# An encoder layer on one core: pair products interleaved, half weight tiles, no full-width GpSimd work, and the switch moved inside attention

## The chip, the cores and the metric

The kernel runs on one core of a Trainium2 chip, in one launch. The metric is the device time in microseconds (us). Five engines take part: PE (TensorE, matrix products into PSUM banks), DVE (VectorE), ACT (ScalarE), POOL (GpSimd) and SP (SyncE, which here only issues transfers). Each works through its own instructions in the order in which the program lists them.

## What is computed

Two sequences of 1024 tokens and 1024 features go through one encoder layer each, in float32. Cut to what matters:

```python
h = rmsnorm(x, norm_g) * (1.0 + scale) + shift          # scale, shift, gate = split(silu(c) @ w_ada + b_ada)
a_b, a_c, a_x, a_z, q, k, v, b_z, lr_f, lr_b, m_a, m_b = split(h @ w_in)
u   = depthwise_conv(a_c * a_x, conv_w, conv_b)
y_a = (a_b * u * silu(a_z)) @ w_a_out
g_f, g_b = log_sigmoid(lr_f @ w_gate_f + b_gate_f) / 16, log_sigmoid(lr_b @ w_gate_b + b_gate_b) / 16
o   = gla(q, k, v, g_f, strict=False) + flip(gla(flip(q), flip(k), flip(v), flip(g_b), strict=True))
y_b = (rmsnorm_per_head(o) * gla_norm_g * silu(b_z)) @ w_b_out
out = rmsnorm(x + gate * ((sigmoid(m_a) * y_a + sigmoid(m_b) * y_b) @ w_out), final_norm_g)
```

## The kernel before, in words

Activations stand transposed: 128 features on the partitions, tokens in the free dimension. A float32 product is made of three: each operand is split into a rounded high part and the rest (`split`, L120: ACT writes the high part, L122, DVE subtracts, L123), and high by high, high by low and low by high are summed in PSUM. One matrix product is then 128x128 weights by 512 tokens.

For each sequence `s` the stages follow each other. `start` (sequence 0 alone) makes the normalised input with the first three projections and ends with `sums` and `sum_parts` of all four activation tiles; `first_conv` finishes their convolution. For sequence 1 `refill` makes the input during the merge before it. `projections` runs **pair jobs**: `fast` (L230) makes two 128-column weight tiles by all tokens with the seven products of the Winograd form of Strassen's scheme, 12 matmuls each. `stationary` (L183) makes the seven stationary operands (six by `split`, the second by L206 to L210) on ACT and DVE, four products ahead (`AHEAD`); in sequence 0 each is also stored to DRAM by SP (L190), and sequence 1 loads it from there (`loaded`, L219). The seven products go to three banks a, b, c in the order a, c, b, a, b, b, c, and five DVE additions (L274, L280, L281, L284, L287) and two ACT copies (L272, L276) read the banks. A raw weight tile of 512 KB takes one of three slots, an operand one of four. Fourteen or sixteen jobs a sequence are convolution channels (`conv_jobs`: C, X, Z, B), where POOL makes the products of `silu` (L637, L649, L673); ten are queries, keys, values and gates, and beside these run `low_ranks` and `decays` (PE, then four ACT functions, each with a table load, L821 to L827) and a third task (`prepare` or `gate_rows`). `small` tiles of 4 KB a partition share seven slots.

`mixers` (L740) runs attention for four heads and fills PE with ordinary products (`halves`): first the 20 of `gates`, spread over three heads; at the start of the fourth `run(dense)` ends them, and `first_out` begins, whose activation `b` `reload` (L1004) brings from DRAM and splits, and spreads its eight products over that head. In attention POOL subtracts the low part of the queries (`Qs`, L919). `merge` multiplies by `w_b_out` (POOL adds at L1024), `final` by `w_out` (POOL subtracts for `mg`). A scheduler sets the order on each engine from the dependences, the slots and the place in the code.

Of the kernel before, what the change touches and what calls it, by code (L numbers as in the profile page):

```python
# [11 lines left out]
F32 = mybir.dt.float32  # L12
# [5 lines left out]
P = 128  # L18
# [17 lines left out]
NBIG, NSMALL, NW, NRAW = 18, 7, 4, 3  # L36
# [21 lines left out]
def encoder_kernel(ctx, tc, x_p, x_s, x_t, weights, w_lr, w_gate, w_out, vectors, b_gate, final_norm_g, masks, y_p, y_s):  # L58
# [52 lines left out]
    r1_d = dram.tile([P, L], F32, name="r1_d")  # L111
    gb_d = dram.tile([2, P, D], F32, name="gb_d")

    def staged(src, shape=(P, L), queue=lambda load: None):

        raw = sb.tile(list(shape), F32, name="raw", tag="raw", bufs=NRAW)
        queue(nc.sync.dma_start(out=raw, in_=src))
        return raw
# [7 lines left out]
    def load_w(i, w=None, **kw):  # L126

        with tc.high_priority(offset=30):
            raw = staged(weights[i].rearrange("p (k c) -> p k c", c=P), (P, KT, P), **kw)
            parts = []  # L130
            for half in range(2):
                t = sb.tile([P, 2, 4, P], F32R, name="w", tag="w", bufs=NW) if w is None else w[:, half]
                split(t[:, 0], t[:, 1], raw[:, 4 * half:4 * half + 4], nc.vector)
                parts.append(t)
        return lambda k: (parts[k // 4][:, 0, k % 4, :], parts[k // 4][:, 1, k % 4, :])
# [47 lines left out]
    def stationary(load, keep=None):  # L183
# [4 lines left out]
        def kept(t, n):  # L188
            if keep is not None:
                nc.sync.dma_start(out=kept_d[keep, n], in_=t.bitcast(F32).rearrange("p a c -> p (a c)"))  # L190
            return t
# [13 lines left out]
        x = sb.tile([P, 4 * P], F32, name="s1", tag="s1", bufs=2)  # L205
# [7 lines left out]
        yield parts(a12, 3)  # L213
        nc.vector.tensor_sub(out=a12, in0=a12, in1=a11)
        yield parts(a21, 4)
# [3 lines left out]
    def loaded(keep):  # L219

        yield None
        for n in range(7):
            if n % 2:
                t = sb.tile([P, 2, 4 * P], F32R, name="wk", tag="raw", bufs=NRAW)
            else:
                t = sb.tile([P, 2, 4 * P], F32R, name="w", tag="w", bufs=NW)
            nc.sync.dma_start(out=t.bitcast(F32).rearrange("p a c -> p (a c)"), in_=kept_d[keep, n])
            yield t

    def fast(jobs, mv):  # L230

        ops = []

        def make():
            later = iter(())
            for n, (load, _, _) in enumerate(jobs):
                gen = later if n else load()
                if not n:  # L240
                    next(gen)
                for i in range(7):
                    if i == 2 and n + 1 < len(jobs):
                        later = jobs[n + 1][0]()
                        next(later)
                    ops.append(next(gen))
                    yield
                next(gen, None)

        maker = make()  # L250
        for load, place, there in jobs:
            banks = {}
            for i, (o, first) in enumerate(((B11, True), (0, True), (1, True), (B21, False), (2, False), (3, False),
                                            (B22, False))):
                while len(ops) < AHEAD[load.ready]:
                    if next(maker, 0) == 0:
                        break
                if first:
                    banks["acb"[i]] = dense_ps()
                a, b, c = (banks.get(n) for n in "abc")  # L260
                ps = banks["acbabbc"[i]]
                w = ops.pop(0)
                for k in range(4):
                    (mhi, mlo), cs = mv.operand(o, k), slice(k * P, (k + 1) * P)

                    nc.tensor.matmul(ps, w[:, 0, cs], mhi, start=(first and k == 0), stop=False, skip_group_check=True)  # L266
                    nc.tensor.matmul(ps, w[:, 0, cs], mlo, start=False, stop=False, skip_group_check=True)  # L267
                    nc.tensor.matmul(ps, w[:, 1, cs], mhi, start=False, stop=(k == 3), skip_group_check=True)  # L268
                if i == 0:
                    keep = small("keep", shape=(P, 2, HALF))  # L270
                    p1, u2 = keep[:, 0, :], keep[:, 1, :]
                    nc.scalar.copy(out=p1, in_=a)  # L272
                elif i == 2:
                    nc.vector.tensor_add(out=u2, in0=b, in1=p1)  # L274
                elif i == 3:
                    nc.scalar.copy(out=place(0, 0), in_=a)  # L276
                    there(0, 0)
                elif i == 4:
                    d = place(1, 1)
                    nc.vector.tensor_add(out=d, in0=b, in1=p1)  # L280
                    nc.vector.tensor_add(out=d, in0=c, in1=d)  # L281
                    there(1, 1)
                elif i == 5:
                    nc.vector.tensor_add(out=place(1, 0), in0=b, in1=p1)  # L284
                    there(1, 0)
                elif i == 6:
                    nc.vector.tensor_add(out=place(0, 1), in0=c, in1=u2)  # L287
                    there(0, 1)
                yield
# [874 lines left out]
```

## Time and profile before

| what | value |
|---|---|
| median of 3 runs | 2523.21 us (2519.05 to 2525.99) |
| the profiled execution's own time | 2527.07 us |
| its span | 2525.3 us |
| PE busy | 2355.0 us (93%), 10993 matmuls |
| DVE, ACT, POOL busy | 1439.7, 999.3, 312.2 us |
| mean granted clock of PE | 0.968 |
| DMA moved | 464.70 MB, mean 184 GB/s |

A matmul of 512 columns shows some 0.4 us, but they are pipelined, so the time from one start to the next is shorter; what PE loses is read from its idle time, the granted clock, and the count of matmuls in a stretch.

### The profile page before, as it was taken

The numbers are of one execution on the slowest core, as the hardware profiler recorded it, in microseconds if no ns is written. First come the engines' busy times: TensorE is split into PE (matmuls) and PEld (weight loads), VectorE is DVE, ScalarE is ACT, GpSimd is POOL, SyncE is SP. The second block draws the span as 40 slices with busy tenths as digits, with TensorE's granted clock in tenths as the row PEclk, the third lists the DMA queues.
The fourth block names the chain that finished last, engine by engine and source line by source line (L and its number), as shares of the span: only waits on it lengthen the run. The fifth ranks groups of instructions, "written<-read, shape, count | busy, mean of one in ns | idle before, by whom it ended". The sixth has DMA issues, their size and how long they took to land.

```text
span 2525.3 us, 28803 instructions
## 1 busy us (share of the span) xinstructions
PE 2355.0 (93%) x10993; PEld 1916.8 (76%) x10993; DVE 1439.7 (57%) x1895; ACT 999.3 (40%) x1579; POOL 312.2 (12%) x187
## 2 busy tenths in 40 slices
PE   7799988989999998999999998998999997999998
PEld 4677766767788876887788886777778886888887
DVE  5866765667766575667732333434857566644333
ACT  6532222786444444343310112772444444332221
POOL 2210110001100100012101110010010000003431
PEclk8899999999999998899999999999999998999999
DMA  6256655768714233437366664777432415358531
GB/s 236 74 218 245 242 208 208 267 253 315 284 64 150 88 122 140 161 134 274 125 199 209 203 209 155 255 252 267 184 115 101 152 67 208 107 202 289 184 127 67
DMA packets 145898, 464.70 MB, mean 184 GB/s; under 512 B 13760, under 2 KB 38944, under 8 KB 142688
## 3 DMA queue, kind: packets, MB, share of 16 engines
q1 hardware_dynamic: 122144, 377.25, 43.3%
q10 hardware_dynamic: 23616, 85.60, 8.6%
q8 instruction: 87, 1.43, 0.2%
q14 instruction: 51, 0.42, 0.1%
HBM read 280.87 MB, written 181.93 MB: 183 GB/s over the span
## 4 chain that ended last, share of the span: by engine, by line
PE 65%; ACT 8%; DVE 8%; DMA 8%; issue 8%; POOL 2%; ACTq 0%; SPq 0%; DVEq 0%; POOLq 0%
PE ps L141 10%; PE ps L143 10%; PE ps L142 10%; PE ps L266 9%; PE ps L268 8%; PE ps L267 8%; DMA raw<-in_weights_dram 4%; PE pl L854 3%; PE pm L141 1%; PE pm L142 1%; PE pm L143 1%; DMA qk<-q_d 1%; DVE w L123 1%; PE ps L788 1%; DMA x<-in_x_t_dram 1%
## 5 line engine op out<-in xcount | busy, mean ns | idle before, releaser
L122 ACT CAST w<-raw 128x512 fp32r<-128x512 f32 x306 | 185.7, 619 | 296.0 <-PE ps L143 108.7
L123 DVE TENSOR_TENSOR w<-raw,w 128x512 fp32r<-128x512 f32 x306 | 231.2, 765 | 119.2 <-ACT w L122 117.3
L141 PE MATMUL ps<-hi,w 128*128 128x512 f32 x688 | 275.4, 402 | 15.0 <-ACT pr L728 9.5
L143 PE MATMUL ps<-hi,w 128*128 128x512 f32 x688 | 274.3, 399 | 0.2 <-DVE w L123 0.2
L142 PE MATMUL ps<-lo,w 128*128 128x512 f32 x688 | 273.3, 397 | 0.0
L266 PE MATMUL ps<-th,w 128*128 128x512 f32 x608 | 247.9, 408 | 25.3 <-DVE single L280 10.9
L268 PE MATMUL ps<-th,w 128*128 128x512 f32 x608 | 243.7, 401 | 12.6 <-DVE w L210 10.9
L267 PE MATMUL ps<-tl,w 128*128 128x512 f32 x608 | 242.9, 399 | 0.0
L141 PE MATMUL ps<-b,w 128*128 128x512 f32 x512 | 204.7, 400 | 12.2 <-ACT w L122 11.4
L266 PE MATMUL ps<-hi,w 128*128 128x512 f32 x504 | 198.2, 393 | 7.9 <-ACT w L122 3.0
L142 PE MATMUL ps<-b,w 128*128 128x512 f32 x512 | 202.9, 396 | 0.0
L143 PE MATMUL ps<-b,w 128*128 128x512 f32 x512 | 200.9, 394 | 0.0
L268 PE MATMUL ps<-hi,w 128*128 128x512 f32 x504 | 196.4, 392 | 1.4 <-DVE w L123 1.4
L267 PE MATMUL ps<-lo,w 128*128 128x512 f32 x504 | 197.6, 392 | 0.1
L266 PEld LDWEIGHTS ps<-th,w 128*128 128x128 f32 x608 | 118.0, 194 | 62.7 <-DVE single L280 15.4
L141 PEld LDWEIGHTS ps<-hi,w 128*128 128x128 f32 x688 | 131.1, 191 | 41.0 <-ACT pr L728 9.9
L143 PEld LDWEIGHTS ps<-hi,w 128*128 128x128 f32 x688 | 131.0, 190 | 26.5 <-DVE w L123 0.6
L142 PEld LDWEIGHTS ps<-lo,w 128*128 128x128 f32 x688 | 131.2, 191 | 24.0
L268 PEld LDWEIGHTS ps<-th,w 128*128 128x128 f32 x608 | 117.4, 193 | 41.8 <-DVE w L210 13.8
L267 PEld LDWEIGHTS ps<-tl,w 128*128 128x128 f32 x608 | 118.2, 194 | 24.0
L141 PEld LDWEIGHTS ps<-b,w 128*128 128x128 f32 x512 | 98.0, 191 | 32.7 <-ACT w L122 12.4
L266 PEld LDWEIGHTS ps<-hi,w 128*128 128x128 f32 x504 | 95.2, 189 | 31.3 <-ACT keep L272 5.0
(271 smaller groups left out, 4687.4 us busy)
## 6 DMA issues: line engine op xcount, KB each, us to landing
kept_d<-w SPq DMA_DIRECT2D x168, 512.0 KB, 3.3
raw<-in_weights_dram SPq DMA_DIRECT2D x128, 512.0 KB, 5.1
w<-kept_d SPq DMA_DIRECT2D x96, 512.0 KB, 4.2
wk<-kept_d SPq DMA_DIRECT2D x72, 512.0 KB, 4.0
g_d<-sg ACTq DMA_DIRECT2D x32, 512.0 KB, 2.7
g<-g_d SPq DMA_DIRECT2D x32, 512.0 KB, 5.4
araw<-in_weights_dram SPq DMA_DIRECT2D x16, 512.0 KB, 4.3
ta_d<-u ACTq DMA_DIRECT2D x16, 512.0 KB, 2.9
```

Source lines behind the costliest of these rows:

```text
L122: high = nc.scalar.copy(out=hi, in_=raw)
L123: engine.tensor_sub(out=lo, in0=raw, in1=hi.bitcast(F32))
L141: nc.tensor.matmul(out, ahi, bhi, start=(first and i == 0), stop=False)
L142: nc.tensor.matmul(out, ahi, blo, start=False, stop=False)
L143: nc.tensor.matmul(out, alo, bhi, start=False, stop=(last and i == n - 1))
L266: nc.tensor.matmul(ps, w[:, 0, cs], mhi, start=(first and k == 0), stop=False, skip_group_check=True)
L267: nc.tensor.matmul(ps, w[:, 0, cs], mlo, start=False, stop=False, skip_group_check=True)
L268: nc.tensor.matmul(ps, w[:, 1, cs], mhi, start=False, stop=(k == 3), skip_group_check=True)
L788: nc.tensor.matmul(ps[:4 * RANK], w[:, k, :], h, start=(k + i == 0), stop=(k * i == KT - 1))
L854: nc.tensor.matmul(pl[:, j * P:(j + 1) * P], km[:, c * P:(c + 1) * P], qm(c), start=True, stop=True)
```

## The change

1. `fast`: the products of neighbouring jobs alternate. In the steady state P1 and P5 of job n are followed by P4 of job n-1, P6 of n, P3 of n-1, P2 and P7 of n. P1, P6, P7 and P4 use one bank, P5 and P3 another, P2 a third; P1 has its bank from `psl`, two banks that attention used alone. Three DVE additions and four ACT copies are left for each job; two 512-wide `keep` tiles stand outside `small`, which has six slots.
2. Raw tiles are half as large (256 KB) in six slots; each half of a weight tile is its own transfer.
3. The products of `silu`, `Ql`, the low part of `mg` and the sum at L1024 go from POOL to DVE.
4. `low_ranks` leaves `decays`: in sequence 0 it follows the product W_AB in `first_conv`, between the calls for sums; in sequence 1 it stands ahead of the first job. Its result goes through DRAM.
5. `mixers`: `gates` and `first_out` form one chain, spread evenly over the four heads; the last two gates, the first two and the last two outputs run as groups of two, feature by feature over four banks (`group`). The steps for keys are halved.

```diff
-NBIG, NSMALL, NW, NRAW = 18, 7, 4, 3
+NBIG, NSMALL, NW, NRAW = 18, 6, 4, 6
...
-        r1, r2 = load(0), None
+        a11, a21 = load(0, 0), load(1, 0)
         yield None
-        r2 = load(1)
-        r1, r2 = (r.rearrange("p k c -> p (k c)") for r in (r1, r2))
-        a11, a12, a21, a22 = r1[:, :HALF], r1[:, HALF:], r2[:, :HALF], r2[:, HALF:]
+        a22, a12 = load(1, 1), load(0, 1)
...
+        P1, P5, P6, P2, P7, P4, P3 = range(7)
+        moving = {P1: B11, P5: 0, P6: 1, P2: B21, P7: 2, P4: 3, P3: B22}
+        steps = [(n - late, i) for n in range(len(jobs) + 1)
+                 for i, late in ((P1, 0), (P5, 0), (P4, 1), (P6, 0), (P3, 1), (P2, 0), (P7, 0))
+                 if 0 <= n - late < len(jobs)]
...
+            first = i in (P1, P5, P2)
+            if first:
+                job[i] = level_ps() if i == P1 else dense_ps()
+            ps = job[{P6: P1, P7: P1, P4: P1, P3: P5}.get(i, i)]
...
+            if i in (P1, P6):
+                job[i, "keep"] = sb.tile([P, HALF], F32, name="keep", tag="keep", bufs=3)
+                nc.scalar.copy(out=job[i, "keep"], in_=ps)
+            elif i == P5:
+                nc.scalar.copy(out=place(1, 1), in_=ps)
+            elif i == P2:
+                nc.vector.tensor_add(out=place(0, 0), in0=ps, in1=job[P1, "keep"])
+                there(0, 0)
+            elif i == P7:
+                nc.vector.tensor_add(out=place(1, 1), in0=ps, in1=place(1, 1))
+                there(1, 1)
+            elif i == P4:
+                nc.scalar.copy(out=place(1, 0), in_=ps)
+                there(1, 0)
+            elif i == P3:
+                nc.vector.tensor_add(out=place(0, 1), in0=ps, in1=job[P6, "keep"])
+                there(0, 1)
...
-            nc.gpsimd.tensor_mul(out=z, in0=z, in1=sg)
+            nc.vector.tensor_mul(out=z, in0=z, in1=sg)
...
+        more = chain(halves(W_AB, lambda ps, sl: nc.scalar.copy(out=pb[:, sl], in_=ps), mv.act), low_ranks(s, mv))
+        next(more)
+        for k in range(4):
+            sums_of(k)
+            next(more, None)
+        run(more)
...
-        dense, todo = gates(), (2 * KT + 4) * 4
-        each = todo / 3.0
+        dense, each = chain(gates(), first_out()), (3 * KT + 4) * 4.0 / NH
         owed = 0.0
         for h in range(NH):
-            if h == NH - 1:
-                run(dense)
-                dense, each = first_out(), KT * 4.0
-                owed = 0.0
...
-        split(Qs[0], Qs[1], Q, nc.gpsimd)
+        split(Qs[0], Qs[1], Q, nc.vector)
...
-            yield n_keys
+                yield n_keys / 2
```

Three places show what the scheduler makes of it.

DVE, in the first jobs of sequence 0, one job's bank reads before: L274, L280, L281, L284 and L287 add from the banks, L206 to L210 make the second operand, L123 subtracts.

```order
L274 TENSOR_TENSOR keep<-ps,keep 128x512
L123 TENSOR_TENSOR w<-raw,w 128x512
L206 TENSOR_TENSOR s_1048<-raw 128x512
L123 TENSOR_TENSOR w<-raw,w 128x512
L208 TENSOR_TENSOR raw<-raw 128x512
L209 TENSOR_TENSOR raw<-s_1048,raw 128x512
L280 TENSOR_TENSOR pair<-ps,keep 128x512
L210 TENSOR_TENSOR w<-s_1048,w 128x512
L281 TENSOR_TENSOR pair<-ps,pair 128x512
L284 TENSOR_TENSOR pair<-ps,keep 128x512
```

And now, where L296 ends job n-1 while L287 and L290 belong to job n:

```order
L296 TENSOR_TENSOR pair<-ps,keep 128x512
L208 TENSOR_TENSOR raw<-s_1092,raw 128x512
L209 TENSOR_TENSOR w<-s_1092,w 128x512
L287 TENSOR_TENSOR pair<-ps,keep 128x512
L124 TENSOR_TENSOR w<-raw,w 128x512
L290 TENSOR_TENSOR pair<-pl,pair 128x512
```

Three reads a job are left, and no two read the same bank one after the other.

PE, where the ordinary products go over to `first_out` (operand `b`), sequence 0, before: the fourth head's own sums (L359, L854) stand between the last gate and the first `b`.

```order
L141 MATMUL ps<-hi,w 128x512
L142 MATMUL ps<-lo,w 128x512
L143 MATMUL ps<-hi,w 128x512
L997 MATMUL pm<-ident,ot 128x128 x8
L359 MATMUL pl<-Xh,ones 128x512 x2
L359 MATMUL pl<-Xl,ones 128x512 x2
L359 MATMUL pl<-Xh,ones 128x512
L359 MATMUL pl<-Xl,ones 128x512
L359 MATMUL pl<-Xh,ones 128x512
L359 MATMUL pl<-Xl,ones 128x512
L854 MATMUL pl<-Q,km 128x128 x8
L141 MATMUL ps<-b,w 128x512
```

And now, where they come in the third head, between its output products:

```order
L142 MATMUL pm<-Vh,As 128x256
L143 MATMUL pm<-Vl,As 128x256
L144 MATMUL pm<-Vh,As 128x256
L142 MATMUL pm<-SBh,Qh 128x256
L143 MATMUL pm<-SBl,Qh 128x256
L144 MATMUL pm<-SBh,Ql 128x256
L142 MATMUL pm<-SF,Qh 128x256
L143 MATMUL pm<-SF,Qh 128x256
L144 MATMUL pm<-SF,Ql 128x256
L142 MATMUL ps<-b,w 128x512
```

The first `b` no longer stands behind a new head's first operands.

ACT, in the first out job of sequence 0 beside `decays`, now (with what each waits for; L858 to L868 are `decays`, L285 is the copy of P5, L696 the store of a finished row):

```order
L293 COPY single<-pl 128x512 [waits PE_49]
L123 CAST w<-raw 128x512 [waits DMAHW7_49,DVE_49]
L696 DMA q_d_90<-single 128x1024 [waits DVE_49,Activation_49]
L866 ACT_TABLE_LOAD
L866 ACTIVATE t_2970<-t_2970 128x1024 [waits DVE_49]
L283 COPY keep<-pl 128x512 [waits PE_49]
L285 COPY single<-ps 128x512 [waits DMAHW6_49]
L858 ACTIVATE t_3108<-pm,vecs 128x512 [waits DMAHW4_49,PE_49]
L868 ACT_TABLE_LOAD
L868 ACTIVATE t_2971<-t_2971 128x1024 [waits DVE_49]
```

The copy of P5 has come ahead of later functions of `decays`, and it waits for a transfer.

## Rows read from the trace of the kernel before

**Rows 1.** The page, busy time of PE over the span.
```profile
PE 2355.0 (93%) x10993; PEld 1916.8 (76%) x10993; DVE 1439.7 (57%) x1895; ACT 999.3 (40%) x1579; POOL 312.2 (12%) x187
```

**Rows 2.** Windows: length, busy us and count of PE, PEld, DVE, ACT, POOL, clock, DMA.
```profile
1300.00:1400.00 100.00, 100.00 (x438) 81.65 (x437) 34.49 (x40) 12.71 (x16) 9.55 (x4) 1.00 0.63 204
2300.00:2526.00 226.00, 217.93 (x985) 181.34 (x983) 78.05 (x101) 45.57 (x90) 67.29 (x59) 0.99 0.43 145
```

**Rows 3.** Windows, pair jobs: first_conv, conv jobs, low_ranks, out jobs; then sequence 1.
```profile
97.00:112.00 15.00, 5.50 (x14) 4.19 (x14) 14.26 (x20) 9.48 (x11) 2.47 (x1) 0.66 0.26 93
112.00:425.00 313.00, 291.22 (x1237) 234.25 (x1235) 209.72 (x258) 90.79 (x143) 38.80 (x16) 0.98 0.61 227
425.00:436.00 11.00, 5.18 (x14) 2.67 (x13) 4.75 (x6) 0.92 (x2) 1.74 (x1) 0.70 0.40 143
436.00:650.00 214.00, 194.68 (x795) 151.21 (x794) 142.68 (x185) 158.05 (x196) 15.44 (x6) 0.95 0.75 277
...
1240.00:1551.00 311.00, 309.04 (x1337) 251.00 (x1337) 105.34 (x129) 43.07 (x60) 36.00 (x16) 0.99 0.59 189
...
1551.00:1780.00 229.00, 208.29 (x865) 163.80 (x865) 97.04 (x112) 124.76 (x138) 16.54 (x7) 0.96 0.71 240
```

**Rows 4.** Windows, the switch in both sequences, and the merges.
```profile
985.00:1024.00 39.00, 23.40 (x93) 18.38 (x92) 31.90 (x35) 19.55 (x27) 2.58 (x2) 0.65 0.64 235
1137.00:1240.00 103.00, 96.84 (x417) 78.75 (x415) 72.31 (x84) 37.95 (x46) 26.53 (x16) 0.98 0.66 234
...
2105.00:2130.00 25.00, 12.79 (x49) 9.29 (x48) 22.48 (x25) 14.36 (x16) 1.53 (x2) 0.66 0.54 192
2251.00:2300.00 49.00, 45.98 (x199) 37.78 (x197) 26.56 (x30) 13.81 (x18) 10.72 (x7) 0.97 0.90 328
```

**Rows 5.** Waits of PE, whole span: us in total, times, longest.
```profile
PE ps L266 <- DVE single L280: 18.5, 8, 5.3
PE pm L933 <- DVE kt L123: 15.3, 8, 2.5
...
PE ps L788 <- DVE wlr L123: 12.4, 2, 6.5
...
PE ps L141 <- ACT pr L728: 9.5, 1, 9.5
```

**Rows 6.** Timeline, POOL and DVE, 178.5 to 186 us: start, length.
```profile
178.91 0.69 DVE L208 TENSOR_TENSOR raw<-raw 128x512 f32<-128x512 f32 x1
178.93 2.92 POOL L637 TENSOR_TENSOR single<-single,pair 128x1024 f32<-128x1024 f32 x1 [61.37 <-ACT pair L636]
...
179.64 2.76 DVE L209 TENSOR_TENSOR raw<-s,raw 128x512 f32<-128x512 f32 x1
```

**Rows 7.** Groups of DVE: count, busy us, mean ns of one.
```profile
L123 DVE TENSOR_TENSOR w<-raw,w 128x512 fp32r<-128x512 f32 x306 | 231.2, 765 | 119.2 <-ACT w L122 117.3 <-DMA kept_d<-w 0.3
...
L123 DVE TENSOR_TENSOR As<-AT,As 128x1024 fp32r<-128x1024 f32 x8 | 30.5, 3817 | 1.2
...
L287 DVE TENSOR_TENSOR single<-ps,keep 128x512 f32<-128x512 f32 x32 | 22.0, 687 | 12.5 <-PE ps L268 12.5
...
L123 DVE TENSOR_TENSOR Xl<-K,Xh 128x2048 fp32r<-128x2048 f32 x8 | 18.3, 2291 | 4.8 <-ACT Xh L122 4.8
...
L652 DVE TENSOR_TENSOR u<-u,single 128x1024 f32<-128x1024 f32 x12 | 14.7, 1225 | 1.0
```

**Rows 8.** Groups of ACT, the same columns.
```profile
L276 ACT COPY single<-ps 128x512 f32<-128x512 f32 x32 | 18.7, 583 | 70.7 <-PE ps L268 70.7
```

**Rows 9.** DMA issues: count, KB each, median us to landing.
```profile
raw<-in_weights_dram SPq DMA_DIRECT2D x128, 512.0 KB, 5.1
...
v_d<-single ACTq DMA_DIRECT2D x16, 512.0 KB, 4.9
...
raw<-in_weights_dram SPq DMA_DIRECT2D x16, 256.0 KB, 5.7
```

More of the change, by code (lines that the diff above doesn't have):

```diff
@@ L111, in encoder_kernel, with staged @@
     r1_d = dram.tile([P, L], F32, name="r1_d")
+    lr_d = [dram.tile([96, L], F32, name=f"lr_d{s}") for s in range(2)]
     gb_d = dram.tile([2, P, D], F32, name="gb_d")
-    def staged(src, shape=(P, L), queue=lambda load: None):
-        raw = sb.tile(list(shape), F32, name="raw", tag="raw", bufs=NRAW)
+    def staged(src, queue=lambda load: None):
+        raw = sb.tile([P, HALF], F32, name="raw", tag="raw", bufs=NRAW)
         queue(nc.sync.dma_start(out=raw, in_=src))
@@ L234, in fast @@
         ops = []
         def make():
[L237 to L248, printed above, removed]
@@ L250, in fast @@
-        maker = make()
[L251 to L289, printed above, removed]
@@ new lines, in make, with begin @@
+            gens = [iter(())] * (len(jobs) + 1)
+            def begin(n):
+                if n < len(jobs):
+                    gens[n] = jobs[n][0]()
+                    next(gens[n])
+            begin(0)
+            for n, i in steps:
+                if i == P6:
+                    begin(n + 1)
+                ops.append(next(gens[n]))
+                yield
+        maker = make()
+        state = [{} for _ in jobs]
+        for n, i in steps:
+            load, place, there = jobs[n]
+            while len(ops) < AHEAD[load.ready]:
+                if next(maker, 0) == 0:
+                    break
+            job = state[n]
+            first = i in (P1, P5, P2)
+            if first:
+                job[i] = level_ps() if i == P1 else dense_ps()
+            ps = job[{P6: P1, P7: P1, P4: P1, P3: P5}.get(i, i)]
+            whi, wlo = ops.pop(0)
+            for k in range(4):
+                (mhi, mlo), cs = mv.operand(moving[i], k), slice(k * P, (k + 1) * P)
+                nc.tensor.matmul(ps, whi[:, cs], mhi, start=(first and k == 0), stop=False, skip_group_check=True)
+                nc.tensor.matmul(ps, whi[:, cs], mlo, start=False, stop=False, skip_group_check=True)
+                nc.tensor.matmul(ps, wlo[:, cs], mhi, start=False, stop=(k == 3), skip_group_check=True)
+            if i in (P1, P6):
[15 more added lines that the diff above has]
+                there(0, 1)
+            yield
@@ L504, in start, with sums_of @@
                 next(features, None)
[L505 removed]
+        def sums_of(k):
             for b in range(2):
@@ L509, in start @@
             mv.sum_parts(k, mv.sums(k, xT[k]))
-        mf = small("mf", shape=(P, len(MASKED), P))
-        nc.sync.dma_start(out=mf, in_=masks)
-        nc.vector.tensor_copy(out=mk, in_=mf)
-        return [[(b[t], slice(t * HALF, (t + 1) * HALF)) for t in range(2)] for b in banks]
+        return [[(b[t], slice(t * HALF, (t + 1) * HALF)) for t in range(2)] for b in banks], sums_of
     def gate_rows():
```

162 lines of the change are left out of this document (98 added, 64 removed).

## The prediction

> **What bounds the kernel now.** I read the page first: PE is busy for 2355.0 of 2525.3 us [rows 1], so PE bounds nearly every stage, and a faster helper is worth only what PE stops waiting. Then the windows give PE's own pace. Where it never waits, 438 matmuls start in 100 us at the full clock [rows 2]: 100 / 438 = 0.228 us each. A stretch made almost wholly of such 512-wide matmuls should last its count times 0.228; the excess is idle time and half clock together. The last stretch confirms it: 985 x 0.228 = 224.9 of 226 us [rows 2]. In the other pair stretches the reader is to see a time well over the count [rows 3]:
>
> - end of the start and first_conv: 15.0 - 14 x 0.228 = 11.8 us;
> - conv jobs of sequence 0: 313 - 1237 x 0.228 = 30.6;
> - low_ranks of sequence 0: 11 - 3.2 = 7.8;
> - out jobs of sequence 0, beside decays: 214 - 181.5 = 32.5;
> - conv jobs of sequence 1: 311 - 305.2 = 5.8;
> - out jobs of sequence 1, low_ranks and gate rows included: 229 - 197.5 = 31.5.
>
> The merges lose 103 - 95.2 = 7.8 and 49 - 45.4 = 3.6 by the same count [rows 4]. At the switch to `first_out` many matmuls are narrow, so I bound the loss: at least the idle time, 39 - 23.4 = 15.6 and 25 - 12.8 = 12.2; at most that plus half of the busy time, if all of it ran at 1.2 GHz (the clock there is 0.65 and 0.66), 27.3 and 18.6 [rows 4]. The waits name who ends what: DVE's addition out of bank b (18.5 us), the second half of the transposed keys (15.3, eight times), low_ranks' weights (12.4, twice), and ACT's copies out of the start's banks (9.5) [rows 5]. All of this comes to 131.4 + 15.3 + 28 to 46 = 175 to 193 us that could at most return.
>
> **The change part by part.**
>
> *Interleaving.* Before, products five and six both write bank b, so PE stands until DVE has added; L280 costs 18.5 us [rows 5]. Now PE returns to a bank after two whole products of others (24 x 0.228 = 5.5 us), against a read of 0.58 on ACT [rows 8] or 0.69 on DVE [rows 7]. Each job sheds two DVE additions (2 x 50 x 0.687 = 69 us of DVE over all jobs) and gains two ACT copies (2 x 50 x 0.583 = 58 us of ACT), both off PE's path if the queues keep up.
>
> *No full-width work on POOL.* First the row: at 178.91 a DVE operation of 512 takes 0.69 us; at 178.93 POOL starts a 1024-wide product, and DVE's next operation, same size but with two SBUF sources, takes 2.76, ending just after POOL [rows 6]. The same shows in the means: `w` 0.765 against 0.687 for reads from PSUM, and `As` 3.817 where 1024 elements otherwise take 1.225 [rows 7]. What moves to DVE is 48 products of 1024 (58.8 us), eight of 2048 (18.3), 16 of 1024 for `mg` (19.6) and 32 of 512 (22.0): 118.7 us. Off go the 68.7 of additions, 306 x 0.078 = 23.9 of waiting in `w` and 8 x 2.59 = 20.7 in `As`: net 5 us more on an engine that is idle for over 1000. What returns is on PE's side: second operands come no longer several us late. The Trainium skill (SBUF — State Buffer, Who interferes with whom) calls the pair of ports that VectorE and GpSimd share an exclusive lock for the whole instruction, which agrees with 2.76 us; it also says that the one that issues first wins, by which the small POOL operations that stay could still delay a DVE operation.
>
> *Half raw tiles.* The four quarters of a job come and go by themselves, so the next job's first two can load while this job's last two are in use. SP issues 2 more transfers a job in sequence 0 (four for two), between the stores that wait for DVE; sequence 1 loads three operands in two pieces. The trace has no contiguous 256 KB load. Bounds: half of the 512 KB row, 2.6 us, and the row for 256 KB in two strided pieces, 5.7 [rows 9]. I take 4, about the middle, since neither row is like it (one is contiguous but twice the size, one is in short pieces); the operand is needed three products after the slot is free, 8.2 us, so all but the upper end is covered, together with the stores.
>
> *Conv jobs together* (three edits above): of 30.6 us in sequence 0 I leave 10, for single late operands and one or two half-clock stretches: -20. Sequence 1 loads its operands: -2.
>
> *Out jobs.* The same, but ACT is the tight engine: 158 busy of 214 [rows 3], now plus 10 x 2 x 0.583 = 11.7 minus a little for low_ranks, about 168 in what should become some 195 us. Its long functions still stand between PE and the splits. I leave 18 of 32.5 in sequence 0 (-14) and, with low_ranks gone, 14 of 31.5 in sequence 1 (-17; low_ranks' own wait of some 6 us and the slow clock behind it are more than half).
>
> *low_ranks and first_conv.* In sequence 0 low_ranks' 64 matmuls (14.6 us) and W_AB's 48 (11.0) now stand where PE waited, while DVE makes the last sums (14.3 of 15 us busy there [rows 3]); the copies out of the start's banks come ahead of ACT's casts. The 7.8 us go, and 9 of 11.8: -17 together. What is late next is wlr's subtraction, behind those sums on DVE; I leave 3 us for it. In sequence 1 it covers the refill's last tile.
>
> *The switch.* The last gates and the first outputs lie between products of the third head, with matmuls of that head to fill in, and `b` loads as the gates give up their activation feature by feature. Of 15.6 to 27.3 and 12.2 to 18.6 I take 20 and 16, since most of the busy time there is at the low clock, and leave 3 each: -30.
>
> *Keys and merges.* The step between the halves of the keys now offers 1 or 2 ordinary products; `As` is 1.2 instead of 3.8, but `Ql` comes to DVE with 2.3, so DVE is hardly earlier: 15.3 becomes 7, -8. The merges lose POOL's sums from their chain: -4, though DVE, 72 of 103 busy, takes 11 us more.
>
> Sum: 20 + 2 + 14 + 17 + 17 + 30 + 8 + 4 = 112; less 7 for groups that hold all four weight slots when they begin: 105. The profiled execution's own time is 2527.07, so 2422; it lies 3.9 over the median of the runs, 2523.21, so the forecast against that median is **2418 us**.
>
> **Rivals.**
>
> *Half loads come late.* Each transfer of half the size costs nearly a whole one [rows 9], SP issues behind stores that wait, and the second pair of quarters is late in every job. The 26 jobs that split their weights (24 in sequence 0, two in sequence 1) would each wait 5.7 - 4 = 1.7 us more, 44 us, and the half clock of the sequence 0 stretches stays, 0.02 x 313 + 0.05 x 214 = 17 [rows 3]: 61 us given back, 2479. Against it: DMA is busy 0.61 and 0.75 in these stretches [rows 3], not full. The Trainium skill (DMA: Bandwidth & Descriptors, Bandwidth) tells authors to batch transfers to 1 MiB or more, because each has a fixed cost near 2 us; by its formula, an estimate, two halves take 5.2 us in turn where one whole takes 3.2. The rows show 5.1 for the whole, so queueing rules here, not that formula.
>
> *ACT's queue stops in the out jobs: slower.* `small` now has six slots. Two hold `decays`' operands, and two overlapping jobs hold four rows, so the copy of P5 waits for a store, with ACT's weight casts queued behind it, and PE behind those. The price is up to a whole store, 4.9 us [rows 9], plus about 2.5 for PE's clock, in each of 20 out jobs: 148 us, against a gain of 105 - 31 = 74 elsewhere: 2597. It decides from a wait of about 3.7 us in each job (74 / 20). For it: the listing shows that copy waiting on a transfer. Against it: a row is finished before the next job's P5 plus two products, and other slots free up between.
>
> *DVE inherits the waits.* In attention and merges DVE has the new work in line, keys and merges gain nothing and the switch half: 2418 + 8 + 4 + 15 = 2445, or 2455 with wlr late too.
>
> *All goes.* Nearly all the excess of pair jobs and switch vanishes: 2523 - 155 = 2368.
>
> *It does nothing.* PE's excess only moves to the next operand, as every pair still needs seven splits on the same two engines: 2520. Against it: those engines are idle for a third in these stretches.
>
> **How the numbers follow.** Forecast 62%, with an own range of 2390 to 2440; late loads 12%; DVE 8%; all goes 10%; ACT stops 5%; nothing 3%. Faster by over 0.3% (7.6 us, about what a measurement of this kernel can tell from no change) is 62 + 12 + 8 + 10 = 92%; within 0.3%: 3%; slower: 5%. The range leaves out ACT's stop, no effect, and part of the case that all goes: 2362 to 2488.
>
> **What would show it.** Right: conv jobs of sequence 0 within 10 us of count x 0.228; no wait for an addition out of the same bank; DVE's `w` near 0.69; the clock near 1.0 at the switch, with PE idle under 4 us. Wrong: PE waiting on ACT's `w` or `keep` in the out jobs with ACT at a bank copy; SP's raw loads landing just before DVE's first sum; PE idle before the first `b`. A pace of PE other than 0.228 us would upset every count.

## The result and the profile after

The changed kernel takes **2380.53 us** (median of 4 runs, 2375.43 to 2382.12) against 2521.56 for the kernel before (4 runs): ratio **0.9435, 95% interval 0.9415 to 0.9456**, 141 us less. The forecast was 2418, in a range of 2362 to 2488. The profiled execution took 2379.61 us with a span of 2377.8; PE's mean granted clock rose from 0.968 to 0.988.

The page, busy time of the changed kernel's span:
```profile
PE 2306.3 (97%) x10993; PEld 1900.6 (80%) x10993; DVE 1411.8 (59%) x1962; ACT 1057.8 (44%) x1731; POOL 60.0 (3%) x83
```
PE runs the same 10993 matmuls [rows 1] and is idle for 72 us instead of 170. POOL lost 252 us of work, yet DVE, which took it over, is busy for 28 us less than before. Not all full-width work has left POOL: the start's nine subtractions for `wa` (1024 wide) stay there, 25 us.

Windows of the changed kernel by stage: the end of the start with first_conv and low_ranks, the conv jobs, the out jobs, the switch, the merge; then from 1148 the same stages of sequence 1 (columns as in [rows 2]):
```profile
69.00:114.00 45.00, 41.92 (x189) 31.46 (x190) 40.51 (x59) 28.39 (x38) 3.96 (x2) 0.92 0.14 51
114.00:399.00 285.00, 285.00 (x1258) 235.69 (x1256) 191.09 (x258) 113.01 (x185) 0.00 (x0) 1.00 0.72 262
399.00:607.00 208.00, 189.21 (x782) 150.30 (x782) 131.95 (x177) 171.34 (x217) 0.00 (x0) 0.96 0.81 295
...
900.00:960.00 60.00, 56.02 (x287) 46.09 (x286) 40.47 (x57) 28.98 (x63) 2.40 (x4) 0.97 0.69 240
...
1070.00:1148.00 78.00, 75.39 (x332) 60.96 (x331) 62.56 (x84) 31.45 (x37) 0.00 (x0) 1.00 0.63 213
1148.00:1450.00 302.00, 300.90 (x1326) 247.69 (x1325) 102.88 (x115) 64.13 (x96) 0.00 (x0) 1.00 0.58 193
1450.00:1655.00 205.00, 196.70 (x845) 160.36 (x845) 88.81 (x107) 130.22 (x150) 0.00 (x0) 0.98 0.80 266
...
1965.00:2020.00 55.00, 50.06 (x254) 41.48 (x253) 38.99 (x56) 25.61 (x53) 2.40 (x4) 0.97 0.77 260
...
2130.00:2196.00 66.00, 66.00 (x293) 54.66 (x292) 38.10 (x54) 19.32 (x28) 0.00 (x0) 1.00 0.86 296
```
The reader is to count as in the prediction, time less matmuls x 0.228. The conv jobs of sequence 0 are at PE's pace: 285 matches 1258 x 0.228 = 286.8, where before 30.6 us were over [rows 3]. Only the out jobs are far from it: 208 - 178.3 = 29.7 us over in sequence 0 (before 32.5) and 205 - 192.7 = 12.3 in sequence 1 (before 31.5).

What PE waits for over the whole span of the changed kernel (us, times, longest):
```profile
PE ps L278 <- ACT w L206: 8.0, 3, 3.7
PE pm L416 <- POOL wa L124: 6.7, 5, 2.3
...
PE pm L1038 <- DVE ot L1030: 5.3, 10, 0.8
PE ps L142 <- ACT w L123: 4.7, 3, 2.3
...
PE pl L278 <- ACT w L123: 4.2, 2, 2.5
PE pl L280 <- DVE w L124: 4.2, 3, 3.0
```
Of the waits in [rows 5] none is left: no bank that DVE still adds out of (18.5 us before), no transposed keys (15.3), no `wlr` (12.4), no `pr` (9.5). What leads now is PE waiting for ACT's cast of a second operand (L206), all three times in the out jobs of sequence 0. The start's waits for `wa` are as they were, outside the change.

The groups of DVE, then the DMA issues, of the changed kernel:
```profile
L124 DVE TENSOR_TENSOR w<-raw,w 128x512 fp32r<-128x512 f32 x306 | 210.4, 693 | 134.1 <-ACT w L123 132.8
...
L124 DVE TENSOR_TENSOR Ql<-Q,Qh 128x2048 fp32r<-128x2048 f32 x8 | 18.3, 2293 | 8.0 <-ACT Qh L123 8.0
...
L124 DVE TENSOR_TENSOR As<-AT,As 128x1024 fp32r<-128x1024 f32 x8 | 9.7, 1215 | 0.0
```
```profile
kept_d<-w SPq DMA_DIRECT2D x168, 512.0 KB, 4.0
raw<-in_weights_dram SPq DMA_DIRECT2D x272, 256.0 KB, 4.0
```
DVE's `w` fell from 765 to 693 ns and `As` from 3817 to 1215 [rows 7]: both had been lengthened by POOL. A half tile lands after 4.0 us, the value the forecast had taken.

### The profile page after: what moved, and what is told of

The parts are those of the page before. It is cut to its first block, busy times and chain, and to the rows that moved or that the text cites. A ratio compares the mean times of both kernels' runs of the same rounds, so it can differ in the third digit from the quotient of the medians.

```text
span 2377.8 us, 29338 instructions
## 1 busy us (share of the span) xinstructions
PE 2306.3 (97%) x10993; PEld 1900.6 (80%) x10993; DVE 1411.8 (59%) x1962; ACT 1057.8 (44%) x1731; POOL 60.0 (3%) x83
## 4 chain that ended last, share of the span: by engine, by line
PE 79%; ACT 8%; DVE 5%; DMA 4%; issue 3%; POOL 1%; SPq 0%; ACTq 0%; POOLq 0%; DVEq 0%
PE ps L142 13%; PE ps L143 13%; PE ps L144 13%; PE pl L278 5%; PE pl L279 5%; PE pl L280 5%; PE ps L278 4%; PE ps L280 4%; PE ps L279 4%; PE pl L895 4%; DMA raw<-in_weights_dram 2%; PE pm L142 1%; PE pm L143 1%; PE pm L144 1%; DMA qk<-q_d 1%
## 5 line engine op out<-in xcount | busy, mean ns | idle before, releaser
L124 DVE TENSOR_TENSOR w<-raw,w 128x512 fp32r<-128x512 f32 x306 | 210.4, 693 | 134.1 <-ACT w L123 132.8
L142 PE MATMUL ps<-hi,w 128*128 128x512 f32 x688 | 273.9, 399 | 4.6 <-ACT hi L388 4.6
L144 PE MATMUL ps<-hi,w 128*128 128x512 f32 x688 | 271.8, 395 | 0.0
L143 PE MATMUL ps<-lo,w 128*128 128x512 f32 x688 | 271.2, 394 | 0.4 <-DVE lo L389 0.4
L123 ACT CAST w<-raw 128x512 fp32r<-128x512 f32 x306 | 188.3, 620 | 166.7 <-PE ps L144 88.7
L142 PE MATMUL ps<-b,w 128*128 128x512 f32 x512 | 202.7, 396 | 4.7 <-ACT w L123 4.7
L278 PE MATMUL pl<-th,w 128*128 128x512 f32 x504 | 198.4, 394 | 2.0 <-ACT keep L283 1.9
L280 PE MATMUL pl<-th,w 128*128 128x512 f32 x504 | 197.1, 391 | 3.0 <-DVE w L124 3.0
L279 PE MATMUL pl<-tl,w 128*128 128x512 f32 x504 | 197.2, 391 | 0.0
L142 PEld LDWEIGHTS ps<-hi,w 128*128 128x128 f32 x688 | 129.8, 189 | 29.7 <-ACT hi L388 5.8
L144 PEld LDWEIGHTS ps<-hi,w 128*128 128x128 f32 x688 | 130.0, 189 | 26.0
L283 ACT COPY keep<-pl 128x512 f32<-128x512 f32 x100 | 58.3, 583 | 194.2 <-PE pl L280 186.2
L278 PE MATMUL ps<-hi,w 128*128 128x512 f32 x304 | 118.4, 390 | 1.1 <-ACT w L123 1.1
L280 PE MATMUL ps<-hi,w 128*128 128x512 f32 x304 | 118.3, 389 | 0.0
L279 PE MATMUL ps<-lo,w 128*128 128x512 f32 x304 | 118.3, 389 | 0.0
L142 PEld LDWEIGHTS ps<-b,w 128*128 128x128 f32 x512 | 97.0, 190 | 24.5 <-ACT w L123 5.5
L278 PEld LDWEIGHTS pl<-th,w 128*128 128x128 f32 x504 | 95.4, 189 | 24.7 <-ACT keep L283 4.4
L280 PEld LDWEIGHTS pl<-th,w 128*128 128x128 f32 x504 | 95.0, 189 | 23.6 <-DVE w L124 3.6
L144 PEld LDWEIGHTS ps<-b,w 128*128 128x128 f32 x512 | 96.9, 189 | 20.0 <-DVE w L124 0.2
```

The lines of the kernel that those rows point to most:

```text
L123: high = nc.scalar.copy(out=hi, in_=raw)
L124: engine.tensor_sub(out=lo, in0=raw, in1=hi.bitcast(F32))
L142: nc.tensor.matmul(out, ahi, bhi, start=(first and i == 0), stop=False)
L143: nc.tensor.matmul(out, ahi, blo, start=False, stop=False)
L144: nc.tensor.matmul(out, alo, bhi, start=False, stop=(last and i == n - 1))
L278: nc.tensor.matmul(ps, whi[:, cs], mhi, start=(first and k == 0), stop=False, skip_group_check=True)
```

## The experiments

Twelve runs beside the result tell the parts apart. Each has its median, then its ratio to the kernel before from runs on the same chip, with the 95% interval; 0.001 is 2.5 us. The changed kernel is at 0.9435. "Over" and "under" compare with its median, 2380.53 us; the runs stand on several chips, so where the two ratios give another difference, it is named too. Such a difference is uncertain by some 6 to 11 us. A "loss" is a stretch's time less its count of matmuls x 0.228.

**What POOL's work costs**, put back into the changed kernel and taken alone out of the old one.

> The changed kernel with the products of silu, the low parts of the queries and of mg, and the merge's sum back on POOL; all else as changed. Lock theory (the conv jobs of sequence 0 lost their 30.6 us because POOL held the port while DVE made second operands): the conv jobs, 285 us at 0.4 us of loss in the changed kernel, lose 15 to 25 us again, merges 4, and the time is 2400 to 2415. Slack theory (interleaving and half tiles give enough slack that a DVE operation of 2.8 us is covered): DVE's w goes back to about 0.77 us but the conv jobs lose under 5 and the time stays within 10 us of 2380.

```diff
-        split(Qs[0], Qs[1], Q, nc.vector)
+        split(Qs[0], Qs[1], Q, nc.gpsimd)
...
-            nc.vector.tensor_mul(out=z, in0=z, in1=sg)
+            nc.gpsimd.tensor_mul(out=z, in0=z, in1=sg)
...
-                nc.vector.tensor_add(out=g[:, sl], in0=m1[:, sl], in1=g[:, sl])
+                nc.gpsimd.tensor_add(out=g[:, sl], in0=m1[:, sl], in1=g[:, sl])
```
(and the other products of the convolutions and `mg`). Measured: 2441.17 us, 0.9674 (0.9638 to 0.9709): 60 us of the gain are given back. Neither theory had the place right, and the time is 26 us over the lock theory's upper end. By the starts of matmuls in the trace, the conv jobs of sequence 0 take 272.5 us from first to last, the changed kernel 266.4: 6 us, where the theory asked for 15 to 25. From the last matmul of the pair jobs to attention's own last one it is 468.0 and 460.8 us in the two sequences, the changed kernel 443.5 and 444.8: 40 of the 60. The wait that came back, and a piece of the timeline where it arises:
```profile
PE pm L974 <- DVE kt L124: 20.3, 8, 2.6
```
```profile
682.37 4.61 POOL L124 TENSOR_TENSOR Ql<-Q,Qh 128x2048 fp32r<-128x2048 f32 x1 [48.71 <-ACT Qh L123]
...
684.24 3.82 DVE L124 TENSOR_TENSOR As<-AT,As 128x1024 fp32r<-128x1024 f32 x1
...
684.59 1.00 ACT L123 CAST kt<-pm 128x512 fp32r<-128x512 f32 x2
...
687.99 1.14 DVE L124 TENSOR_TENSOR kt<-pm,kt 128x512 fp32r<-128x512 f32 x2
688.72 0.69 PE L974 MATMUL pm<-ident,K 128*128 128x128 f32 x2 [2.54 <-DVE kt L124]
```
Read it downwards: POOL's `Ql` runs until 686.98; DVE's `As` starts in its midst and ends at 688.06, 1.08 us after POOL, about as long as it takes undisturbed (1.215); `kt`, whose casts are done by 685.6, stands behind it; PE waits 2.54 us.

> The kernel before with only the full-width POOL work moved to DVE (five additions a job, whole raw tiles, old order). Lock theory: the conv jobs of sequence 0 fall from a loss of 30.6 to 10 or less, As to 1.2 us, time 2480 to 2495. Slack theory: DVE is only busier (no additions are shed), the conv jobs still lose 20 or more, time 2505 to 2520. A slower time than before (2530) would say that DVE's extra work is itself on the path.

The edit is the same seven places in the kernel before, `nc.gpsimd` to `nc.vector`. Measured: 2474.38 us, 0.9805 (0.9749 to 0.9862): 49 us, by the interval 35 to 63 (two runs, 11 us apart), for moving work between two engines that PE hardly seemed to wait for. It is 6 us under the lock theory's range, and its other two signs came: DVE's `As` takes 1.216 us, and the conv jobs of sequence 0 take 275.0 us from first to last matmul, before 298.0, which leaves 6.9 over 1176 x 0.228. No wait for `kt` is left, though the keys are still one step; attention, counted as above, takes 462.3 and 460.2 us, before 471.5 and 468.1. So POOL's work cost the conv jobs 23 us in the old kernel and 6 in the changed one, whose other parts leave them more slack, and attention 17 in the old and 40 in the changed. What is left names the next limits:
```profile
PE pl L854 <- ACT km L882: 12.7, 2, 6.6
PE pl L359 <- ACT Xh L122: 12.1, 5, 4.8
PE ps L141 <- ACT w L122: 11.5, 4, 3.5
PE ps L788 <- DVE wlr L123: 11.2, 2, 6.6
PE ps L141 <- ACT pr L728: 9.5, 1, 9.5
PE ps L266 <- DVE single L280: 9.2, 4, 4.6
```
The first three lines lie for the most part in the two switches (12.7, 8.8 and 6.3 us of them); then come low_ranks and the start's banks, and only the last is the bank that the interleaving frees.

**Interleaving.**

> The changed kernel with the pair products in the old order: one job at a time, three banks, five additions, keep in small with seven slots; half tiles, no POOL work, low_ranks and the switch as changed. If the interleaving carries the gain of the pair jobs, PE waits again for an addition out of bank b, some 15 to 20 us over all jobs, and the conv jobs lose 15 or more: 2415 to 2440. If the lock carried it, the conv jobs lose under 8 and the time is 2390 to 2405.

The edit puts `fast` of the kernel before into the changed one, with operands in two pieces and seven small slots. Measured: 2383.95 us, 0.9447 (0.9419 to 0.9474), 3 us over: under the ranges of both theories, and no difference clear of noise. The conv jobs of sequence 0 stay within 2 us of PE's pace, and the out jobs are even shorter. Its windows of these two stages:
```profile
116.00:398.00 282.00, 281.61 (x1230) 229.08 (x1228) 209.00 (x284) 97.73 (x153) 0.00 (x0) 1.00 0.72 262
398.00:602.00 204.00, 191.99 (x808) 153.09 (x808) 145.24 (x198) 159.38 (x197) 0.00 (x0) 0.97 0.83 306
```
204 - 808 x 0.228 = 19.8 us over, against 29.7: the old order has two ACT copies fewer a job, ACT is busy for 159 instead of 171 us. What the old order loses elsewhere is about as much, 6.5 us of it in the out jobs of sequence 1 (217.0 us from first to last matmul, changed 210.5). Waits at the bank that DVE adds out of, 18.5 us before [rows 5], come to 9.2 in the run with only POOL's work moved and to 6.1 here: more than half of what the interleaving was to free went with POOL.

**Half tiles.**

> The changed kernel with before's order of the seven products and whole raw tiles again (three slots of 512 KB, whole kept tiles, whole reloads); same raw memory, GpSimd, low ranks and switch as changed. To be held against the run with before's order and half tiles (2384 us). Of the 90 us between that run and the one with only the GpSimd work moved (2474), the switch gave 35 and the low ranks 26 when undone alone; 29 are unassigned. If half tiles carry them, this run gives 2405 to 2415 us, with new waits in the convolution jobs of sequence 0. Rival: raw slots were no limit once GpSimd was gone, 2380 to 2390 us, and the 29 us are an interplay of the other parts. I expect 2390 to 2400.

```diff
-NBIG, NSMALL, NW, NRAW = 18, 7, 4, 6
+NBIG, NSMALL, NW, NRAW = 18, 7, 4, 3
...
-        a11, a21 = load(0, 0), load(1, 0)
-        yield None
-        a22, a12 = load(1, 1), load(0, 1)
+        r1, r2 = load(0), None
+        yield None
+        r2 = load(1)
```
(shown against the run before, whose order it keeps; kept tiles and reloads whole as well). Measured: 2402.82 us, 0.9523 (0.9504 to 0.9542), 19 us over 2383.95: just under the 2405 that the theory of the half tiles asked, 13 over the rival's upper end and 3 over what I expected. Windows of the same two stages:
```profile
115.00:402.00 287.00, 282.77 (x1231) 229.23 (x1229) 207.15 (x283) 96.26 (x153) 0.00 (x0) 1.00 0.69 257
402.00:612.00 210.00, 195.46 (x809) 153.78 (x808) 146.25 (x200) 160.04 (x198) 0.00 (x0) 0.97 0.80 299
```
5 and 6 us of it are here; most of the rest is in the attention of sequence 0 (5) and the out jobs of sequence 1 (3). Whole tiles in three slots under the interleaved order were not tried: a job's first operands then need a slot that the job before frees only later.

**The switch.**

> The changed kernel with the ordinary products spread as before: gates over three heads, then all ended and first_out begun at the start of the fourth; groups of two kept. If the place of the switch carries the gain there, PE idles 10 to 15 us at low clock before the first b in both sequences and the time is 25 to 35 us longer, 2405 to 2415. If the gain came from groups and the DVE free of the lock, under 10 us.

```diff
-        dense, each = chain(gates(), first_out()), (3 * KT + 4) * 4.0 / NH
+        dense, each = gates(), (2 * KT + 4) * 4 / 3.0
...
+            if h == NH - 1:
+                run(dense)
+                dense, each = first_out(), KT * 4.0
+                owed = 0.0
```
Measured: 2415.30 us, 0.9571 (0.9534 to 0.9609), 35 us over. The waits that return, in the first sequence's switch (900 to 980 us):
```profile
PE ps L142 <- ACT w L123: 9.9, 1, 9.9
PE pl L368 <- ACT Xh L123: 4.7, 1, 4.7
```
The pair stands once more in sequence 1 (9.3 and 4.8): 28.7 us of waits, with four shorter ones for `Xl` and `AT` 33.3. From 920 to 960 us PE's clock is 0.78 and 0.71 in two windows of 20 us; the changed kernel has 0.91 and 1.00 there.

**low_ranks and the start's sums.**

> The changed kernel with low_ranks back in decays in both sequences and the start's sums back ahead of the copies out of its banks. If these two carried the gain between the start and the conv jobs and at the head of the out jobs: PE idles some 9 us at the end of the start and some 6 us ahead of low_ranks in each sequence, with half-clock stretches behind: 20 to 28 us longer, 2400 to 2408. If the rest of the change would have covered them: under 8 us longer.

```diff
-            run(low_ranks(s, mv))
...
-        side = chain(decays(s), gate_rows() if s else prepare())
+        side = chain(decays(s, mv), gate_rows() if s else prepare())
...
+        for k in range(4):
+            sums_of(k)
...
+        run(low_ranks(lrs, mv))
```
Measured: 2406.48 us, 0.9548 (0.9520 to 0.9576), 26 us over, by the ratios 28. In 107 to 410 us, up to the out jobs of sequence 0, 1247 matmuls take 303 us, 18.7 over their count; PE waits there for
```profile
PE ps L825 <- DVE wlr L124: 10.0, 1, 10.0
PE pl L280 <- DVE w L124: 4.5, 1, 4.5
```
Half of what was expected did not come: no wait at the end of the start returned (`pr`, 9.5 us before), and ahead of `low_ranks` of sequence 1 PE waits 2.0 us, not 6. So most of the price is that of `low_ranks` in sequence 0; this run doesn't show which part of the change freed the start's banks.

**Keys.**

> The changed kernel with the transposed keys of a direction in one step again, as before: no products between their halves. The forecast gave this part 8 us, on before's eight waits of the transposes for kt (15.3 us). The run with only the GpSimd work moved has none of those waits although its keys are in one step, and the run with GpSimd's work back has them all (20.3 us) although they are in two. So I expect now that the waits were GpSimd's, and the step alone carries 0 to 3 us: 2378 to 2384 us, kt waits under 3 us. Rival, the forecast's reason: without products in between the transposes wait again, 6 to 15 us in kt, 2386 to 2394 us.

```diff
-                yield n_keys / 2
+            yield n_keys
```
Measured: 2381.12 us, 0.9421 (0.9404 to 0.9438), no difference clear of noise, and not one wait for `kt`. The eight waits of [rows 5] were POOL's.

**What holds the out jobs.**

> The changed kernel with the stores of the operands for sequence 1 issued from POOL's queue instead of SP's, so that a raw load no longer stands behind a store that waits for DVE. Load theory for what the out jobs of sequence 0 still lose (30 us in 399 to 607 us): the loss falls to 15 or less, time 2362 to 2370. ACT theory: it stays at 25 to 32, time within 5 us of 2380. A rise would say that issuing from POOL itself costs DVE or the transfers.

```diff
-                nc.sync.dma_start(out=kept_d[keep, n], in_=t.bitcast(F32).rearrange("p a c -> p (a c)"))
+                nc.gpsimd.dma_start(out=kept_d[keep, n], in_=t.bitcast(F32).rearrange("p a c -> p (a c)"))
```
Measured: 2393.79 us, 0.9498 (0.9470 to 0.9525), slower by 13, by the ratios 16, of which 8 are in the attention of sequence 0. The out jobs are no shorter: 209 us for 778 matmuls from 402 to 611 us, a loss of 31.6. Taking the stores out of SP's queue did not bring the raw loads earlier: in these jobs DVE waits for one at its first sum (L205) eight times, 16.8 us, where it was four times and 9.5. But the run has a price of its own, POOL busy for 33.6 us there, so it doesn't settle what late loads cost.

> The changed kernel with all four functions of decays replaced by one that the gates' silu uses too, so that the decay values are wrong and nearly all table loads (1.28 us each, 64 in both sequences) fall away; the same instructions otherwise. ACT theory: the out jobs of sequence 0 lose 12 us or less instead of 30 and those of sequence 1 a few us less; time 2355 to 2365. Load theory: the loss stays at 22 or more; time 2372 to 2380.

```diff
-                nc.scalar.activation(out=t1, in_=t1, func=AF.Exp, scale=-1.0)
-                nc.scalar.activation(out=t1, in_=t1, func=AF.Ln, bias=1.0)
+                nc.scalar.activation(out=t1, in_=t1, func=AF.Sigmoid, scale=-1.0)
+                nc.scalar.activation(out=t1, in_=t1, func=AF.Sigmoid, bias=1.0)
```
(and the other two functions the same way). Measured: 2358.00 us, 0.9356 (0.9328 to 0.9383), 22.5 us under the changed kernel, by the ratios 20. Its window of the out jobs of sequence 0:
```profile
398.00:584.00 186.00, 179.59 (x778) 146.72 (x779) 128.47 (x172) 118.58 (x174) 0.00 (x0) 0.99 0.90 329
```
186 - 778 x 0.228 = 8.6 us over instead of 29.7: the ACT theory holds, and 21 us of the loss are the table loads'. In these jobs of the changed kernel ACT loads a table 39 times (eight times at each of the four functions of `decays`, six at the sigmoid, one elsewhere), 1.28 us each: 50 us. What one such burst does there, in the timeline of the changed kernel:
```profile
482.86 0.60 ACT L123 CAST w<-raw 128x512 fp32r<-128x512 f32 x1
...
483.48 1.28 ACT L645 ACT_TABLE_LOAD   x1
...
484.77 1.06 ACT L645 ACTIVATE sg<-single 128x1024 f32<-128x1024 f32 x1
...
485.85 1.28 ACT L866 ACT_TABLE_LOAD   x1
...
487.04 0.39 PE L280 MATMUL pl<-hi,w 128*128 128x512 f32 x1
487.15 1.06 ACT L866 ACTIVATE t<-t 128x1024 f32<-128x1024 f32 x1
...
488.22 1.28 ACT L868 ACT_TABLE_LOAD   x1
...
489.51 1.06 ACT L868 ACTIVATE t<-t 128x1024 f32<-128x1024 f32 x1
490.48 0.60 ACT L206 CAST w<-s 128x512 fp32r<-128x512 f32 x1
...
491.13 0.79 PE L278 MATMUL ps<-th,w 128*128 128x512 f32 x1 [3.71 <-ACT w L206]
```
Three functions in a row, each with its table, take ACT from 483.48 to 490.5: 7 us in which no operand is cast. PE runs dry at 487.4, and goes on 0.65 us after the next cast starts. That is not all of the price. The window behind it (clock 0.50) holds 11 matmuls in 5 us, where at full clock there would be 22:
```profile
491.00:496.00 5.00, 4.87 (x11) 3.64 (x12) 4.37 (x6) 3.97 (x8) 0.00 (x0) 0.50 0.58 207
```
Of the three waits for L206 in these jobs this is the only one behind a burst. The other two, 2.11 and 2.15 us, begin with a raw load that lands late, and DVE's sum and ACT's cast follow it; the first of them:
```profile
557.99 0.69 DVE L205 TENSOR_TENSOR s<-raw 128x512 f32<-128x512 f32 x1 [1.57 <-DMA raw<-in_weights_dram]
...
558.71 0.62 ACT L206 CAST w<-s 128x512 fp32r<-128x512 f32 x1 [0.82 <-DVE s L205]
...
559.38 0.50 PE L278 MATMUL ps<-th,w 128*128 128x512 f32 x1 [2.11 <-ACT w L206]
```
In the run without table loads the longest wait that is left, 3.2 us, is of this kind too. So late loads are a second cause in these jobs, the smaller one: 4.3 of 18.6 us of PE's waits there.

**Three versions that try to use this.**

> The changed kernel with the decays of both directions of a head in step (Exp, Exp, Ln, Ln, ...), which halves their table loads from 64 to 32. If the table loads on ACT's queue hold the out jobs of sequence 0 (the run without them gained 22.5 us), half of that: 2366 to 2372 us, and a loss of about 18 to 22 us left in those jobs. Rival: what counts is the length of one burst in ACT's queue, and two functions in a row make it no shorter: 2376 to 2384 us.

> The changed kernel with the two copies that drain P5 and P4 on DVE instead of ACT in the jobs that write q, k, v and z, of both sequences. That takes 20 copies of 0.58 us = 12 us off ACT in the 208 us of sequence 0's jobs, where ACT is busy 171 us and DVE 132. If ACT's amount of work holds these jobs: 2368 to 2373 us. If it is the bursts of table loads alone, the copies merely move: 2376 to 2381 us. If DVE's queue is the next to be late: 2381 to 2388 us.

> Both of the two edits before together. If ACT's queue is the one limit left in the jobs that write q, k, v and z: 2358 to 2366 us, near the 2358 of the run without table loads. If the two give the same microseconds twice: no better than the better of the two.

```diff
+            for _, t1, t2 in rows:
+                nc.scalar.activation(out=t1, in_=t1, func=AF.Exp, scale=-1.0)
+            yield
+            for _, t1, t2 in rows:
+                nc.scalar.activation(out=t1, in_=t1, func=AF.Ln, bias=1.0)
...
-                nc.scalar.copy(out=place(1, 1), in_=ps)
+                (nc.vector.tensor_copy if load.relief else nc.scalar.copy)(out=place(1, 1), in_=ps)
```
(`rows` holds both directions of a head, and the other two functions go the same way; the last line is the second edit, the same for P4.) Measured: 2375.61 us, 0.9418 (0.9402 to 0.9434); 2376.79, 0.9422 (0.9408 to 0.9436); both together 2374.96, 0.9410 (0.9396 to 0.9424). All three lie under the changed kernel's 0.9435, and their intervals reach into its own, so the best of them is at most a candidate: 6 us. The out jobs of sequence 0 with both edits:
```profile
400.00:598.00 198.00, 186.31 (x777) 147.65 (x778) 139.78 (x191) 141.10 (x181) 0.00 (x0) 0.97 0.84 307
```
20.8 us over instead of 29.7, with ACT down from 171 to 141 us. Each missed the range of its own theory and came out at the near end of the rival's: the first edit takes 15 of 39 loads, 19 us of ACT, out of these jobs, and the time falls by 5; the second takes 12 us off ACT, for 4; both together are no better than either within their intervals. Whether the length of one burst ahead of a cast counts for more than the sum of ACT's work isn't shown. In the windows of the out jobs the loss falls by 21.1 us for 52.8 off ACT without table loads (0.40 us for each), by 5.8 for 19.8 with tables in pairs (0.29), by 5.5 for 12.5 with the copies moved (0.44) and by 8.9 for 30.2 with both (0.29). The copies, which shorten no burst, give as much for each as the loads. A run that breaks up the bursts and leaves ACT its work was not made.

## Why the prediction was right, point by point

Direction and mechanism held, and the time is within the range of 2362 to 2488. It is 9.5 us under the forecast's own range, 2390 to 2440: 36 us more came than the 105 forecast, as the balance of misses both ways. The terms, in the order of the text:

| term | forecast | measured | from |
|---|---|---|---|
| conv jobs, sequence 0 | 20 | 31 | 285 against count x 0.228 |
| conv jobs, sequence 1 | 2 | 6 | 302 against 302.3 |
| out jobs, sequence 0 | 14 | 3 | 32.5 to 29.7 |
| out jobs, sequence 1 | 17 | 19 | 31.5 to 12.3 |
| low_ranks and first_conv | 17 | 18 | 19.6 to 45 - 189 x 0.228 = 1.9 |
| switch | 30 | 35 | undone alone (34 by the ratios) |
| keys | 8 | 0 | undone alone |
| the rest of attention | 0 | 16 | see below |
| merges | 4 | 10 | 11.4 to 78 - 75.7 and 66 - 66.8, so 1.5 |
| groups | -7 | not undone | PE's waits at L142 for ACT's `w` are 4.7 in all; part of the other rows |

"The rest of attention": from the last matmul of the pair jobs to its own last one, attention took 471.5 and 468.1 us before, 443.5 and 444.8 now, with the same count of matmuls within two: 51 us less, of which the switch is 35. The rows come to 138.

**Conv jobs of sequence 0: right step, mis-sized.** The step "of 30.6 I leave 10, for single late operands and one or two half-clock stretches" left too much: nothing late remained, and with no wait there is no slow clock behind it (1.00, before 0.98). What freed them is POOL for the most part: moved alone in the old kernel, it took 23 of the 30 us.

**Out jobs of sequence 0: the step that failed.** "ACT is the tight engine" was right and so was its load, 168 forecast and 171.3 measured, but "I leave 18 of 32.5" credited 14 us to what hardly acts there. In the trace of before, PE's waits at banks in these jobs (436 to 650 us) were 4.7 us in all, and those for ACT's casts 9.2. The interleaving takes away the bank's waits and pays with two ACT copies a job, on the one engine that holds PE; the run without table loads shows 21 us of the loss to be those loads'. The old order is 10 us better in this stage than the new.

**Keys: the right waits, the wrong cause.** "The step between the halves now offers 1 or 2 ordinary products ... -8": the waits went, 15.3 to none, but by way of POOL. The sentence that `As` becomes 1.2 instead of 3.8 (measured 1.215) had the cause in hand, and its next half, "DVE is hardly earlier", dropped it. `Ql` costs DVE 2.293 us, as forecast; but POOL's 4.6 and the 2.6 lost in `As` are gone, and the keys come in time even in one step.

**POOL.** The step "net 5 us more on an engine that is idle for over 1000" expected DVE to work a little more; it worked 28 us less. The profit was put into the conv jobs alone; in attention nothing was credited but the keys. Measured, it is the largest single part: 49 us alone in the old kernel (17 of them in attention), 60 lost when put back into the new (40 in attention).

**Interleaving.** "L280 costs 18.5 us" read the wait rightly, but more than half of it was POOL's to free; undone alone, the interleaving is worth 3 us, which can't be told from none.

**low_ranks.** "In sequence 0 low_ranks' 64 matmuls (14.6 us)" counts both sequences: the trace has 32 in each, 7.3 us. No term of the sum rests on it.

**Half tiles** came as forecast: the load is 4.0 us, and the rival "half loads come late" (2479) fell with it. That 4 was hit so well is partly luck, since it was the middle between two rows that were like neither; that queueing makes the 5.1 of a whole tile, as the rival says, no run shows. **Switch** and **out jobs of sequence 1** were within 5 us; of the signs, "PE idle under 4 us" at the switch came in sequence 0 (4.0) and not quite in sequence 1 (4.9).

Of the rivals, "ACT's queue stops" named the place that stays slow but not the cause: it put a store there, and ACT waits for none in these jobs; it is functions with their tables and, less so, the late raw loads that stood among the signs of being wrong. "DVE inherits the waits" fell: PE waits nowhere for `Ql`, the convolutions' products or the merges' sums. "All goes" (2368) came nearest of all.

The parts add up: 60 (POOL), 35 (switch), 26 to 28 (low_ranks and sums), 19 (half tiles, undone on top of the old order), 3 (interleaving), 0 (keys), 143 to 145 of 141. That the sum fits owes something to chance, since each is uncertain by some 7 to 11 us, and POOL's part is 49 or 60 by the side it is taken from.

## What to carry to other kernels

When two engines contend for a resource, cost the contention at the engine that waits in line behind it, not at the pair: look up what stands in the slowed engine's queue next, and who waits for that. An edit that frees one wait by adding work to another engine should be priced stage by stage, since the same copies are free where that engine is 40% busy and cost some 5 us (the copies moved) to 10 (the old order) where it is 82% busy. Idle time on PE is paid a second time when the clock falls behind it, as after the 3.7 us above, so a few long waits can matter more than the busy share says.

## What the runs showed of the hardware

The switch of ACT's function has a price that is seen in the timeline above: 1.28 us for the load, with the function starting 0.01 to 0.02 us after its end. The Trainium skill (ScalarE: Activation LUTs, What ACT_TABLE_LOAD costs) gives the same 1283 ns and adds a drain of about 1380, some 2.66 us for each switch; here no such gap stands before or after a load, and the rows decide. The Trainium skill (ScalarE: Activation LUTs, Table sets: the hidden batching unit) says that one set holds both the exponential and the logarithm; here every alternation between them loads a table, in both sequences 16 times at each of the four functions, and no run shows how one load for both would be had.

An `As` of 1.215 us that starts within POOL's `Ql` ends 1.08 or 1.09 us after `Ql` does, all eight times in the run with POOL's work back and all eight in the kernel before. So it waits out the rest of POOL's instruction: at half speed beside it, it would need 2.43 us and be done within the 2.74 that `Ql` still takes. And contiguous loads of 256 KB land after 4.0 us where those of 512 KB took 5.1 [rows 9]; the runs with the old order and half or whole tiles have 4.1 and 5.1. Half the bytes cost some 0.8 of the time.
